# Experts with at most 32 tokens: four column quarters of TensorE in place of two halves

## The chip, the cores and the metric

One core of a Trainium2 chip runs the whole program in one launch. The metric is the device time of that launch in microseconds; the time before is the median of 3 runs. One further execution was recorded by the hardware profiler, and all rows below are from it.

## The reference, cut to what matters

Two layers, each a mixer and a feed-forward part, on 256 tokens of width 1024 in float32. The second layer's feed-forward part is a mixture of 8 experts with two chosen per token. The change touches that part alone:

```python
D_MODEL, SEQ, N_EXPERTS, TOP_K, D_FF_EXPERT = 1024, 256, 8, 2, 3584

def moe_swiglu(h, router_w, w_gate, w_up, w_down):
    logits = (xf @ router_w).astype(jnp.float32)
    top_val, top_idx = lax.top_k(logits, TOP_K)
    weights = jax.nn.softmax(top_val, axis=-1)
    ...
    def expert_block(args):
        toks, e = args
        xb = xf[toks]
        return (jax.nn.silu(xb @ w_gate[e]) * (xb @ w_up[e])) @ w_down[e]
    ...
    out = jnp.zeros((N, D), h.dtype).at[row_tok].add(y)
```

Each expert has 3 x 1024 x 3584 float32 weights, 44 MB; all eight are 352 MB, and every one of them is used in every launch.

## The kernel before, in words

`route` (L1090) computes the router's logits, the two chosen experts of each token, each token's place among its expert's tokens (`pos`, counted from 1, 0 where the expert is not chosen), its weight (`comb`) and the number of tokens of each expert (`cnt`). `moe` (L1219) does the rest.

**Steps.** The hidden width of 3584 is cut into ND = 7 pieces of 512, and a step (L1161) is one expert e and one piece d: first experts 0 to 3 for d = 0 to 6 in turn (28 steps: the first group), then experts 4 to 7 (the second group). Four steps of the same d are called a round here. A step needs six tiles of weights of 128 x 2048 float32 (1.0486 MB each): four "g" tiles (gate and up columns side by side: for each of 8 slices of the 1024 inputs and each half `ch` of the piece, 256 gate and 256 up columns) and two "d" tiles (down).

**Blocks.** Tokens of an expert are taken in blocks b of SL = 64; block 0 always runs, further ones under `tc.If(n_of[e] > 64 * b)`. n_of is the expert's count, loaded into registers of TensorE (PE), ScalarE (ACT) and VectorE (DVE) at d = 0 (L1404), behind the first `up` of that expert.

- `up` (L1265): for 8 slices kc and 2 halves ch, the gathered tokens (128 x 64, stationary) times 512 columns of a g tile, added up in one bank of PSUM. Half ch goes to partitions 64 ch to 64 ch + 63, so the two halves use different halves of the array's columns. 16 matmuls in float32, which the profile shows as 32 records. Then ACT computes Silu of the gate half, and DVE multiplies by the up half.
- `turn` (L1278): two transposes of 128 x 128 on PE and a copy by ACT, so that the hidden values lie with the piece's columns on the partitions.
- `down` (L1286): 8 matmuls (16 records) of these (128 x 64, stationary) by the d tiles, again in two halves of the array (n, the two halves of the 1024 outputs); DVE adds the result to `ya`, the expert's output so far.
- `gather` and `gather_more` (L1240, L1253) bring the expert's tokens together by matmuls with 0/1 matrices (`places`); `slots`, `weights` and `scatter` (L1305 to L1331) bring the outputs back at d = 6, with a matrix that holds `comb` at `pos`.

**Order.** The order of PE, ACT and DVE is the order of the program. Step i runs: `up(i, 0)`; `bring(i - 1)` (L1340), which is `down` of the step before, under `tc.If(n_of > 64)` with its further blocks and under `Else` alone; `turn(i, 0)`; then the further blocks' `up` under `tc.If` at L1424. An engine that skips a body takes a branch (COMPARE_BRANCH) and raises its semaphore by what the body would have (EVENT_SEMAPHORE), behind its own earlier work.

**Tiles.** `Stream` (L1164) loads the tiles on the queue of SyncE (SP) in the fixed order g(i), d(i - 1), g(i + 1), ... into 12 buffers (6 `wraw` and 6 `wmore`), which is two steps' worth. `used` (L1213) frees d(i - 1) behind `bring` and g(i) at the end of step i, behind L1424's body; then the next tiles are issued. So the six tiles g(i + 2) and d(i + 1) are issued at the end of step i, where PE's sequencer has passed L1424.

Of the kernel before, what the change touches and what calls it, by code (L numbers as in the profile page):

```python
# [27 lines left out]
NE = 8  # L28
# [11 lines left out]
def block_kernel(ctx, tc, x, cols, rows, ada_w, w_tok, w_in, cmp_w1, cmp_w2, w_out,  # L40
# [9 lines left out]
    def bank(tag, bufs):  # L50
        return pp.tile([128, 512], FT, name=tag, tag=tag, bufs=bufs)
# [7 lines left out]
    def tbank():  # L59
        return bank("tr", 2)  # L60

    def sbank():
        return bank("sc", 2)
# [196 lines left out]
    g = {}  # L260
# [829 lines left out]
    def route(mp, join, hT):  # L1090
        h2 = con.tile([128, 2, D], FT, name="h2", tag="hh")
        lgp = ring()

        def logits(t):
            for kc in range(KC):
                pe.matmul(lgp[:, t * 8:t * 8 + 8], hT[:, kc, t * 128:(t + 1) * 128], rw[:, kc],
                          start=kc == 0, stop=kc == KC - 1)

        def back(t):

            for n in range(2):
                ps = sbank()
                for c in range(4):
                    pe.transpose(ps[:, c * 128:(c + 1) * 128], hT[:, 4 * n + c, t * 128:(t + 1) * 128], ident)
                (act.copy, dve.tensor_copy)[n](h2[:, t, n * 512:(n + 1) * 512], ps)

        join.turn(0)
        join.total(1)
        join.hand(0)
        join.scale(1)  # L1110
        logits(0)
        back(0)
        join.turn(1)
        join.hand(1)
        logits(1)
        v8 = mp.tile([128, 2, 8], FT, name="v8")
        i8 = mp.tile([128, 2, 8], U32, name="i8")
        for t in range(2):
            lg = lgp[:, t * 8:t * 8 + 8]
            dve.max(v8[:, t], lg)  # L1120
            dve.max_index(i8[:, t], v8[:, t], lg)
        idf = mp.tile([128, 2, 8], FT, name="idf")
        dve.tensor_scalar(idf, i8, 1.0, None, op0=OP.add)
        four = [128, 2, 2, NE]
        oh = mp.tile(four, FT, name="oh")
        dve.tensor_tensor(oh, iota_f[:, None, None, 0:8].to_broadcast(four),
                          idf[:, :, 0:2, None].to_broadcast(four), op=OP.is_equal)
        routed = mp.tile([128, 2, NE], FT, name="routed")
        dve.tensor_tensor(routed, oh[:, :, 0], oh[:, :, 1], op=OP.add)
        back(1)  # L1130
        ps = ring()
        pv = ps[:, 0:32].rearrange("p (z t e) -> p z t e", z=2, t=2)
        pe.matmul(pv[:, 0], upper, routed, start=True, stop=False)
        pe.matmul(pv[:, 0, 1], ones, routed[:, 0], start=False, stop=False)
        pe.matmul(pv[:, 1], ones, routed, start=False, stop=True)
        ew = mp.tile([128, 2, 2], FT, name="ew")
        sw = mp.tile([128, 2], FT, name="sw")
        dve.tensor_tensor(ew, v8[:, :, 0:2], v8[:, :, 0:1].to_broadcast([128, 2, 2]), op=OP.subtract)
        act.activation(ew, ew, AF.Exp)

        pos = con.tile([128, 2, NE], FT, name="pos")
        dve.tensor_tensor(pos, pv[:, 0], routed, op=OP.mult)
        total = mp.tile([128, NE], FT, name="total")
        dve.tensor_copy(total, pv[:, 1, 0])
        dve.tensor_tensor(total, total, pv[:, 1, 1], op=OP.add)
        cnt = con.tile([1, NE], I32, name="cnt")
        dve.tensor_copy(cnt, total[0:1])
        comb = con.tile([128, 2, NE], FT, name="comb")

        def shares():  # L1150
            dve.tensor_tensor(sw, ew[:, :, 0], ew[:, :, 1], op=OP.add)
            dve.reciprocal(sw, sw)
            dve.tensor_tensor(ew, ew, sw[:, :, None].to_broadcast([128, 2, 2]), op=OP.mult)
            dve.tensor_tensor(oh, oh, ew[:, :, :, None].to_broadcast(four), op=OP.mult)
            dve.tensor_tensor(comb, oh[:, :, 0], oh[:, :, 1], op=OP.add)

        return h2, pos, comb, cnt, shares

    ND = FFE // 512

# [55 lines left out]
                    self.free[k] = True  # L1216
            self.pump()

    def moe(mp, stream, h2, pos, comb, cnt, shares):  # L1219
        engs = [EN.PE, EN.Activation, EN.DVE]  # L1220
        g2h = mp.tile([128, 512], FT, name="g2h")
        SL = 64
# [1 line left out]
        own = con.tile([128, 2, 2, 2, S], FT, name="own", tag="hl")  # L1224
        uown = own[:, 1].rearrange("p a b c -> p (a b) c")
        hown = con.tile([128, 4, S], FT, name="hown", tag="acc")
        gbank = [lambda: bank("g0", 1), lambda: bank("g1", 1)]
        ebank = [None, lambda: ybank(0), lambda: ybank(1), lambda: ybank(0)]

# [35 lines left out]
        def up(i, b):  # L1265
            e, d = STEPS[i]
            ps = ebank[b]() if b else gbank[i % 2]()
            for kc in range(KC):
                x = xs[e][:, kc, b * SL:(b + 1) * SL]
                for ch in range(2):  # L1270
                    pe.matmul(ps[ch * 64:ch * 64 + 64], x, stream.at["g", i, 2 * (kc // 4) + ch][:, kc % 4],  # L1271
                              start=kc == 0, stop=kc == KC - 1)
            h = hown[:, b] if b or i % 2 else mp.tile([128, 256], FT, name="hid")
            act.activation(h, ps[:, 0:256], AF.Silu)  # L1274
            dve.tensor_tensor(h, h, ps[:, 256:512], op=OP.mult)  # L1275
            hid[i, b] = h

        def turn(i, b):  # L1278
            ps = tbank()
            for f in range(2):  # L1280
                pe.transpose(ps[:, f * 128:(f + 1) * 128], hid[i, b][:, f * 128:(f + 1) * 128], ident)
            u = uown[:, b] if b or i % 2 else mp.tile([128, 256], FT, name="u")
            act.copy(u, ps[:, 0:256])
            us[i, b] = u.rearrange("p (f s) -> p f s", f=2)

        def down(i, b):  # L1286

            e, d = STEPS[i]
            ps = sbank()
            for ch in range(2):  # L1290
                for f in range(2):
                    for n in range(2):
                        pe.matmul(ps[n * 64:n * 64 + 64], us[i, b][:, f, ch * 64:ch * 64 + 64],  # L1293
                                  stream.at["d", i, ch][:, f, n * 512:(n + 1) * 512],
                                  start=ch + f == 0, stop=ch + f == 2)
            ya = yas[e][:, b]
            if d == 0:
                dve.tensor_copy(ya, ps)
            else:
                dve.tensor_tensor(ya, ya, ps, op=OP.add)  # L1300
            if d == ND - 1:
                dve.tensor_tensor(ya, ya, g2h, op=OP.mult)  # L1302


        def slots(e, b):  # L1305

            woh = mp.tile([128, 2, 2, SL], FT, name="woh")
            for t in range(2):
                dve.tensor_scalar(woh[:, t], iota_f[:, None, b * SL:(b + 1) * SL].to_broadcast([128, 2, SL]),
                                  pos[:, t, e:e + 1], comb[:, t, e:e + 1], op0=OP.is_equal, op1=OP.mult)  # L1310
            return woh

        def weights(e, b, woh):
# [26 lines left out]
        def bring(p):  # L1340

            e, d = STEPS[p]

            def back(b):
                if d == ND - 1:
                    scatter(e, b, 0, ybanks)
                    scatter(e, b, 1, sbanks)

            def more(b):
                turn(p, b)  # L1350
                down(p, b)
                back(b)

            with tc.If(n_of[e] > SL) as two:  # L1354
                turn(p, 1)
                down(p, 0)
                down(p, 1)
                back(1)
                beyond(e, more, 2)
            with two.Else():  # L1360
                down(p, 0)
            stream.used("d", p)

        def beside(i, b):

            e, d = STEPS[i]
            if d == ND - 1:
                woh = slots(e, b)
            up(i, b)
            if d == ND - 1:  # L1370
                weights(e, b, woh)

        def g2_row():
# [7 lines left out]
                          dg[:, 4 * n:4 * n + 4].rearrange("p a b -> p (a b)"), start=True, stop=True)  # L1381
            act.copy(g2h, ps)

        gather(0, places(0))
        shares()
        N = len(STEPS)
        done = None
        for i in range(N):
# [8 lines left out]
            if d == ND - 1:  # L1397
                if not e % 4:
                    wx = con.tile([128, 4, S], FT, name="wx", tag="xn0")
                woh = slots(e, 0)  # L1400
            if i < N - 1:
                up(i, 0)
            if d == 0:
                n_of[e] = nc.values_load(cnt[0:1, e:e + 1], engines=engs, min_val=0, max_val=S)  # L1404
            if i == 0:
                gather(2, oh)

# [4 lines left out]
            if i == 4 * ND:  # L1412
                oh = places(6)
            if i == N - 1:
                up(i, 0)
            turn(i, 0)
            if d == ND - 1:
                weights(e, 0, woh)
            if done is not None:
# [1 line left out]
                done = None  # L1421
            if i and STEPS[p][1] == ND - 1:
                done = STEPS[p][0]
            with tc.If(n_of[e] > SL):  # L1424
                if d == 0:
                    gather_more(e)
                beside(i, 1)
                beyond(e, lambda b: beside(i, b), 2)
            stream.used("g", i)
            if i == 5:  # L1430
                g2_row()
# [215 lines left out]
```

## Time and profile before

| | |
|---|---|
| median of 3 runs | 1604.83 us (1600.37 to 1605.38) |
| profiled execution: its time | 1605.7 us |
| its span, first to last instruction | 1604.0 us |
| TensorE matmul busy | 1461.9 us, 91% of the span, 7198 records |
| VectorE, ScalarE busy | 592.2 us (37%), 364.7 us (23%) |
| HBM read | 478.79 MB, 299 GB/s over the span |
| experts (L1219 on) | about 606 to 1604 us |

Instructions carry the kernel's line, their engine and the tiles that they write and read (out<-in). `wraw` and `wmore` are weight tiles, `x` the gathered tokens, `g` and `y` the PSUM banks of `up` for block 0 and for further blocks, `sc` that of `down`, `tr` that of `turn` (and of small products), `hid`, `hown` and `u`, `own` the hidden values before and after the turn. PEld is the loading of stationary operands. PEq is PE's sequencer: a wait that ends with it ends with a branch or a semaphore event there. The span's end follows the last tiles; matmul ends are modelled, and their starts are what to go by.

### The profile page before, as it was taken

How to read it: one execution, taken by the hardware profiler on the slowest of the kernel's cores; microseconds unless marked ns; L12 is line 12 of the kernel's file. 1: busy time of each engine (PE TensorE's matmuls, PEld its weight loads, DVE VectorE, ACT ScalarE, POOL GpSimd, SP SyncE). 2: the span in 40 equal slices, each digit the busy share in tenths (PEclk: the TensorE clock that was granted, in tenths of full speed). 3: DMA queues.
4: the chain of work that ended last, by engine and by line, in shares of the span. 5: the costliest groups of instructions: out<-in, count | busy, mean ns of one | idle time of the engine just before them, and what ended most of it. 6: DMA issues, size and time to landing. Idle time of an engine off the chain costs nothing. (4 is left out here: it accounts for less than half of the span.)

```text
span 1604.0 us, 18623 instructions
## 1 busy us (share of the span) xinstructions
PE 1461.9 (91%) x7198; PEld 791.7 (49%) x7198; DVE 592.2 (37%) x1097; ACT 364.7 (23%) x767; POOL 22.1 (1%) x62
## 2 busy tenths in 40 slices
PE   3999989999898999899999999998989999999985
PEld 3977767887787775233333333333333333333331
DVE  8868767877777751001010110113310100101123
ACT  2656453433574531000000000000000000000000
POOL 2000000000000000000000000000000000000000
PEclk9999999999999989999999999999999999999998
DMA  9745647777465353597889879786969999999992
GB/s 372 286 168 183 210 157 289 298 310 287 176 208 195 132 210 132 228 377 302 367 362 371 360 314 419 307 355 249 401 235 413 418 416 416 403 418 418 398 388 81
DMA packets 67452, 482.40 MB, mean 301 GB/s; under 512 B 7604, under 2 KB 7988, under 8 KB 9288
## 3 DMA queue, kind: packets, MB, share of 16 engines
q1 hardware_dynamic: 66800, 479.66, 75.3%
q8 instruction: 130, 2.13, 0.5%
q14 instruction: 50, 0.41, 0.1%
q10 hardware_dynamic: 472, 0.21, 0.0%
HBM read 478.79 MB, written 1.05 MB: 299 GB/s over the span
## 5 line engine op out<-in xcount | busy, mean ns | idle before, releaser
L1271 PE MATMUL g<-wraw,x 128*64 128x512 f32 x896 | 219.8, 606 | 23.3 <-PEq L1424 10.2
L1271 PE MATMUL g<-wmore,x 128*64 128x512 f32 x896 | 218.0, 600 | 18.6 <-DMA wmore<-in_moe_gu_w_dram 11.3
L1293 PE MATMUL sc<-wraw,own 128*64 128x512 f32 x768 | 172.3, 595 | 3.9 <-ACTq L1335 3.1
L190 DVE TENSOR_TENSOR wlo<-wraw,whi 128x2048 fp32r<-128x2048 f32 (+1 forms) x69 | 153.0, 2230 | 12.2 <-ACT whi L185 12.2
L1271 PEld LDWEIGHTS g<-wraw,x 128*64 128x64 f32 x896 | 73.8, 138 | 142.9 <-issue 121.6
L1271 PEld LDWEIGHTS g<-wmore,x 128*64 128x64 f32 x896 | 73.3, 138 | 141.5 <-issue 118.4
L185 ACT CAST whi<-wraw 128x2048 fp32r<-128x2048 f32 (+1 forms) x69 | 126.8, 1862 | 12.4 <-DMA wraw<-in_w_tok_dram 8.1
L379 PE MATMUL g<-whi,hh 128*128 128x512 f32 (+1 forms) x272 | 112.8, 415 | 8.2 <-DVE hh L371 7.7
L1300 DVE TENSOR_TENSOR ya<-ya,sc 128x512 f32<-128x512 f32 x66 | 45.4, 688 | 187.5 <-PE sc L1293 187.5
L380 PE MATMUL g<-whi,hl 128*128 128x512 f32 (+1 forms) x272 | 108.6, 399 | 0.9 <-DVE hl L372 0.9
L381 PE MATMUL g<-wlo,hh 128*128 128x512 f32 (+1 forms) x272 | 108.1, 397 | 0.3 <-DVE wlo L190 0.3
L1293 PE MATMUL sc<-wmore,u 128*64 128x512 f32 x432 | 107.2, 594 | 0.0
L1293 PEld LDWEIGHTS sc<-wraw,own 128*64 128x64 f32 x768 | 56.6, 137 | 102.5 <-issue 94.2
L1275 DVE TENSOR_TENSOR hown<-hown,g 128x256 f32<-128x256 f32 x28 | 11.8, 421 | 256.2 <-ACTq L1354 185.5
L224 DVE SCALAR_TENSOR_TENSOR acc<-wraw,csil,acc 128x1024 f32<-128x1024 f32 x82 | 105.2, 1283 | 2.2
L1275 DVE TENSOR_TENSOR hid<-hid,g 128x256 f32<-128x256 f32 x28 | 11.8, 421 | 199.4 <-ACT hid L1274 120.1
L379 PE MATMUL g<-hh,whi 128*128 128x256 f32 x256 | 74.7, 292 | 5.5 <-DVE x L526 5.0
L1271 PE MATMUL y<-wraw,x 128*64 128x512 f32 x336 | 76.4, 597 | 0.5 <-DVE ya L1300 0.5
L1271 PE MATMUL y<-wmore,x 128*64 128x512 f32 x336 | 75.7, 592 | 0.0
L380 PE MATMUL g<-hh,wlo 128*128 128x256 f32 x256 | 72.7, 284 | 0.6 <-DVE wlo L190 0.6
L381 PE MATMUL g<-hl,whi 128*128 128x256 f32 x256 | 72.6, 284 | 0.0
L1293 PEld LDWEIGHTS sc<-wmore,u 128*64 128x64 f32 x432 | 40.6, 137 | 56.4 <-issue 47.0
(347 smaller groups left out, 1643.7 us busy)
## 6 DMA issues: line engine op xcount, KB each, us to landing
wraw<-in_moe_gu_w_dram SPq DMA_DIRECT2D x112, 1024.0 KB, 10.3
wmore<-in_moe_gu_w_dram SPq DMA_DIRECT2D x112, 1024.0 KB, 11.2
wmore<-in_moe_d_dram SPq DMA_DIRECT2D x56, 1024.0 KB, 17.3
wraw<-in_moe_d_dram SPq DMA_DIRECT2D x56, 1024.0 KB, 19.8
wraw<-in_ada_w_dram SPq DMA_DIRECT2D x48, 1024.0 KB, 5.3
wraw<-in_w_in_dram SPq DMA_DIRECT2D x24, 1024.0 KB, 4.9
wraw<-in_ffn_gu_dram SPq DMA_DIRECT2D x22, 1024.0 KB, 5.4
wraw<-in_ffn_d_dram SPq DMA_DIRECT2D x11, 1024.0 KB, 4.9
```

The source lines that it names most:

```text
L185: act.copy(self.wh, self.v)
L190: dve.tensor_tensor(self.wl, self.v, self.wh.bitcast(FT), op=OP.subtract)
L224: dve.scalar_tensor_tensor(acc, v[:, o], sc, acc, op0=OP.mult, op1=OP.add)
L379: pe.matmul(ps, ah, bh, start=start, stop=False)
L380: pe.matmul(ps, al, bh, start=False, stop=False)
L381: pe.matmul(ps, ah, bl, start=False, stop=stop)
L1271: pe.matmul(ps[ch * 64:ch * 64 + 64], x, stream.at["g", i, 2 * (kc // 4) + ch][:, kc % 4], start=kc == 0, stop=kc == KC - 1)
L1275: dve.tensor_tensor(h, h, ps[:, 256:512], op=OP.mult)
L1293: pe.matmul(ps[n * 64:n * 64 + 64], us[i, b][:, f, ch * 64:ch * 64 + 64], stream.at["d", i, ch][:, f, n * 512:(n + 1) * 512], start=ch + f ...
L1300: dve.tensor_tensor(ya, ya, ps, op=OP.add)
```

## The change

The count of an expert selects between two forms of block 0, at run time and in every step. With more than 32 tokens the step is as before. With at most 32:

- `up_few`: the same 16 matmuls of 512 columns with 32 tokens as the stationary operand (128 x 32). Half ch and the parity of the slice kc choose one of four quarters of the array's columns, so even and odd slices add up in different partitions of the bank. ACT and DVE copy the bank's two halves to `hid` and `low`, without Silu and product.
- `turn_few`: four matmuls by `sel` (128 x 64, two identities of 32 for each half), which turn the values and add the even and the odd sums; then Silu and the product.
- `down_few`: 8 matmuls in four quarters (output half n, piece half ch); the two ch halves stay apart in `ya`, and the matrix of `slots` holds `comb` at `pos` and at `pos` + 32 (`pos2`), so that `scatter` adds them.

New control flow: `first` (If/Else around `up`), a second If/Else in `bring`, an If/Else around `turn` and L1424's body. The register load at d = 0 moves ahead of `up`. `turn` moves into the new If, behind `weights` and `scatter` in the steps that have them. Buffers, the order of the tiles and their release stay.

```diff
+        pos2 = con.tile([128, 2, NE], FT, name="pos2")
...
         def shares():
+
+            few = mp.tile([128, NE], FT, name="few")
+            dve.tensor_scalar(few, total, 32.0, 32.0, op0=OP.is_le, op1=OP.mult)
+            dve.tensor_tensor(pos2, pos, few[:, None, :].to_broadcast([128, 2, NE]), op=OP.add)
...
+        sel = mp.tile([128, 2, 32], FT, name="sel")
+        iv = ident.rearrange("p (c k s) -> p c k s", c=2, k=2)
+        dve.tensor_tensor(sel, iv[:, :, 0], iv[:, :, 1], op=OP.add)
...
-            h = hown[:, b] if b or i % 2 else mp.tile([128, 256], FT, name="hid")
+            h = hown[:, b] if b else hid[i, 0]
...
-            u = uown[:, b] if b or i % 2 else mp.tile([128, 256], FT, name="u")
+            u = uown[:, b] if b else uof[i]
...
+        def up_few(i):
+
+            e, d = STEPS[i]
+            ps = gbank[i % 2]()
+            for k in range(4):
+                for odd in range(2):
+                    kc = 2 * k + odd
+                    for ch in range(2):
+                        j = 2 * ch + odd
+                        pe.matmul(ps[32 * j:32 * j + 32], xs[e][:, kc, 0:32],
+                                  stream.at["g", i, 2 * (kc // 4) + ch][:, kc % 4], start=k == 0, stop=k == 3)
+            act.copy(hid[i, 0], ps[:, 0:256])
+            dve.tensor_copy(low[i], ps[:, 256:512])
+
+        def turn_few(i):
+
+            ps = tbank()
+            for c in range(4):
+                v = (hid[i, 0] if c < 2 else low[i])[:, c % 2 * 128:(c % 2 + 1) * 128]
+                pe.matmul(ps[:, 64 * c:64 * c + 64], v, sel.rearrange("p c s -> p (c s)"), start=True, stop=True)
+            u = uof[i][:, 0:128]
+            act.activation(u, ps[:, 0:128], AF.Silu)
+            dve.tensor_tensor(u, u, ps[:, 128:256], op=OP.mult)
+
+        def down_few(i):
+            e, d = STEPS[i]
+            ps = sbank()
+            u = uof[i][:, 0:128].rearrange("p (f c s) -> p f c s", f=2, c=2)
+            for f in range(2):
+                for n in range(2):
+                    for ch in range(2):
+                        j = 2 * n + ch
+                        pe.matmul(ps[32 * j:32 * j + 32], u[:, f, ch], stream.at["d", i, ch][:, f, n * 512:(n + 1) * 512],
+                                  start=f == 0, stop=f == 1)
+            gain(i, 0, ps)
...
@@ -1293,6 +1338,10 @@
                         pe.matmul(ps[n * 64:n * 64 + 64], us[i, b][:, f, ch * 64:ch * 64 + 64],
                                   stream.at["d", i, ch][:, f, n * 512:(n + 1) * 512],
                                   start=ch + f == 0, stop=ch + f == 2)
+            gain(i, b, ps)
+
+        def gain(i, b, ps):
+            e, d = STEPS[i]
...
-                dve.tensor_scalar(woh[:, t], iota_f[:, None, b * SL:(b + 1) * SL].to_broadcast([128, 2, SL]),
-                                  pos[:, t, e:e + 1], comb[:, t, e:e + 1], op0=OP.is_equal, op1=OP.mult)
+                for k in range(2):
+                    dve.tensor_scalar(woh[:, t, :, 32 * k:32 * k + 32],
+                                      iota_f[:, None, b * SL + 32 * k:b * SL + 32 * k + 32].to_broadcast([128, 2, 32]),
+                                      (pos2 if k > b else pos)[:, t, e:e + 1], comb[:, t, e:e + 1],
+                                      op0=OP.is_equal, op1=OP.mult)
...
-                down(p, 0)
+                with tc.If(n_of[e] > 32) as one:
+                    down(p, 0)
+                with one.Else():
+                    down_few(p)
...
+        def first(i):
+            with tc.If(n_of[STEPS[i][0]] > 32) as half:
+                up(i, 0)
+            with half.Else():
+                up_few(i)
...
-            if i < N - 1:
-                up(i, 0)
+            hid[i, 0] = hown[:, 0] if i % 2 else mp.tile([128, 256], FT, name="hid")
+            uof[i] = uown[:, 0] if i % 2 else mp.tile([128, 256], FT, name="u")
+            low[i] = mp.tile([128, 256], FT, name="low")
             if d == 0:
                 n_of[e] = nc.values_load(cnt[0:1, e:e + 1], engines=engs, min_val=0, max_val=S)
+            if i < N - 1:
+                first(i)
...
-            turn(i, 0)
+                first(i)
...
-            with tc.If(n_of[e] > SL):
-                if d == 0:
-                    gather_more(e)
-                beside(i, 1)
-                beyond(e, lambda b: beside(i, b), 2)
+            with tc.If(n_of[e] > 32) as half:
+                turn(i, 0)
+                with tc.If(n_of[e] > SL):
+                    if d == 0:
+                        gather_more(e)
+                    beside(i, 1)
+                    beyond(e, lambda b: beside(i, b), 2)
+            with half.Else():
+                turn_few(i)
```

## Rows read from the trace of the kernel before

**Rows 1.** windows: us, busy us (records) of PE, PEld, DVE, ACT, POOL, PEclk, DMA share, GB/s

```profile
606.00:671.00 65.00, 60.08 (x300) 26.00 (x298) 9.08 (x23) 7.03 (x16) 0.00 (x0) 1.00 0.41 163
671.00:1112.00 441.00, 411.95 (x1838) 147.60 (x1838) 54.19 (x103) 29.34 (x78) 0.00 (x0) 1.00 0.84 344
1112.00:1195.00 83.00, 75.19 (x374) 32.76 (x376) 20.18 (x38) 6.50 (x17) 0.00 (x0) 1.00 0.80 318
1195.00:1565.00 370.00, 346.02 (x1528) 124.69 (x1524) 42.75 (x79) 25.02 (x66) 0.00 (x0) 0.99 0.99 408
```

**Rows 2.** timeline, PE, one round: start, us, instruction, records, [idle <-releaser]

```profile
867.70 3.65 PE L1271 MATMUL g<-wmore,x 128*64 128x512 f32 x16 [0.45 <-PEq L1335]
...
874.72 0.44 PE L1281 MATMUL tr<-ident,hown 128*128 128x128 f32 x2
...
887.34 0.41 PE L1281 MATMUL tr<-ident,hid 128*128 128x128 f32 x2 [0.63 <-PEq L1335]
887.90 3.65 PE L1271 MATMUL g<-wraw,x 128*64 128x512 f32 x16
...
909.98 1.04 PE L1271 MATMUL g<-wraw,x 128*64 128x512 f32 x2 [0.15 <-PEq L1424]
911.50 3.22 PE L1271 MATMUL g<-wraw,x 128*64 128x512 f32 x13 [0.48 <-DMA wraw<-in_moe_gu_w_dram]
...
916.47 3.22 PE L1271 MATMUL g<-wmore,x 128*64 128x512 f32 x13 [1.31 <-DMA wmore<-in_moe_gu_w_dram]
...
923.48 0.44 PE L1281 MATMUL tr<-ident,hown 128*128 128x128 f32 x2
...
938.25 3.65 PE L1271 MATMUL g<-wmore,x 128*64 128x512 f32 x16 [0.44 <-PEq L1335]
```

**Rows 3.** timeline, the queue's issues of tiles in the same round

```profile
887.88 0.80 SPq L1201 DMA_DIRECT2D wmore<-in_moe_gu_w_dram  x2
...
909.95 0.80 SPq L1201 DMA_DIRECT2D wmore<-in_moe_gu_w_dram  x2
...
937.93 0.81 SPq L1201 DMA_DIRECT2D wraw<-in_moe_gu_w_dram  x2
...
958.38 0.80 SPq L1201 DMA_DIRECT2D wmore<-in_moe_gu_w_dram  x2
```

**Rows 4.** lines by form: shapes, records | busy us, mean ns | idle before

```profile
L1271 PE MATMUL g<-wraw,x 128*64 128x512 f32 x896 | 219.8, 606 | 23.3 <-PEq L1424 10.2 <-DMA wraw<-in_moe_gu_w_dram 9.0 <-issue 2.3
...
L1271 PE MATMUL y<-wraw,x 128*64 128x512 f32 x336 | 76.4, 597 | 0.5 <-DVE ya L1300 0.5
...
L1275 DVE TENSOR_TENSOR hown<-hown,g 128x256 f32<-128x256 f32 x28 | 11.8, 421 | 256.2 <-ACTq L1354 185.5 <-ACT hown L1274 70.7
...
L281 PE MATMUL tr<-dg,ones 128*128 128x512 f32 x8 | 3.8, 602 | 0.6 <-ACTq L1335 0.6
...
L618 PE MATMUL tr<-kc__323,qT 128*128 128x32 f32 x16 | 1.9, 270 | 0.0
...
L601 PE MATMUL tr<-hs,w 128*64 128x16 f32 x8 | 0.6, 220 | 0.0
```

**Rows 5.** timeline, PE: four records of 16 columns

```profile
137.31 0.29 PE L601 MATMUL tr<-hs,w 128*64 128x16 f32 x4
```

**Rows 6.** lines L1424 and L1404 on TensorE's sequencer: ns min/median/max, first and last start

```profile
L1424 PEldq COMPARE_BRANCH  x56: 70/382/4114, 616.1 to 1581.0; - x56
...
L1404 PEldq TENSOR_LOAD <-cnt x8: 299/309/489, 608.8 to 1199.0; - x8
L1404 PEldq FUSED_REGOPS  x8: 146/146/160, 609.4 to 1199.4; - x8
```

**Rows 7.** timeline, PE: first round, and where the second group settles

```profile
606.12 7.09 PE L1271 MATMUL g<-wraw,x 128*64 128x512 f32 x32
...
671.06 1.51 PE L1271 MATMUL g<-wraw,x 128*64 128x512 f32 x6 [3.11 <-PEq L1424]
...
1194.68 1.94 PE L1271 MATMUL g<-wraw,x 128*64 128x512 f32 x4 [3.89 <-PEq L1424]
```

More of the change, by code (lines that the diff above doesn't have):

```diff
@@ L1155, in shares @@
             dve.tensor_tensor(comb, oh[:, :, 0], oh[:, :, 1], op=OP.add)
-        return h2, pos, comb, cnt, shares
+        return h2, pos, pos2, comb, cnt, shares
     ND = FFE // 512
@@ L1217, in used, with moe @@
             self.pump()
-    def moe(mp, stream, h2, pos, comb, cnt, shares):
+    def moe(mp, stream, h2, pos, pos2, comb, cnt, shares):
         engs = [EN.PE, EN.Activation, EN.DVE]
@@ L1382, in g2_row @@
             act.copy(g2h, ps)
+        def first(i):
[3 more added lines that the diff above has]
+                up_few(i)
+        uof, low = {}, {}
         gather(0, places(0))
@@ L1414, in moe @@
             if i == N - 1:
-                up(i, 0)
-            turn(i, 0)
+                first(i)
             if d == ND - 1:
```

## The prediction

> **What bounds the kernel now.** The windows come first [rows 1]. Up to 606 us this is the mixer, the dense layer and the routing, which the change leaves alone; behind it are the experts. In 671 to 1112 (experts 0 to 3, d = 1 to 6) TensorE is busy 411.95 of 441 us and the transfers run at 344 GB/s; in 1195 to 1565 (experts 4 to 7, from d = 1 on) they run at 408 GB/s with a DMA share of 0.99. So the second group of experts waits for HBM, whatever TensorE does, and in the first TensorE looks like the bound.
>
> How many experts are "few"? The reference's router on its own inputs gives 14, 187, 27, 39, 11, 121, 55 and 58 tokens. The trace agrees: beside 2 x 896 matmul records for the first 64 tokens of all 56 steps stand 2 x 336 for further blocks [rows 4], that is 21 blocks of 32 records, 7 x (2 + 1): three blocks for expert 1 and two for expert 5. Experts 0, 2 and 4 are few: 21 steps of 56, and 14 of them in the first group.
>
> Now one round of the first group, expert by expert [rows 2, 3]. Steps end where the queue issues the next six tiles: expert 2 at 887.88, expert 1 at 937.93, expert 2 again at 958.38. A round takes 70.50 us. One tile takes 2.485 us: TensorE waited for the second and the fourth tile of one step until 911.50 and 916.47. So 24 tiles want 59.6 us, and the round has 10.9 us more. These lie where expert 1's three blocks hold their tiles until the step's end: after the issues at 909.95 the next is at 937.93. From 887.88 on, in contrast, the queue works through a chain of 12 tiles (gate/up of expert 0, down of 3, gate/up of 1, down of 0). Its tenth landed at 916.47, 28.59 us after the chain's start, so the twelfth lands at 28.59 + 2 x 2.485 = 33.56. Expert 1's step already waits for tiles (0.48 and 1.31 us): the half round from 887.88 to 937.93 is bound by transfers and by expert 1, the other (937.93 to 958.38, expert 2) by TensorE alone. That decides what a saving is worth.
>
> **The change part by part.** *Up.* 32 records stay 32, each with 512 columns. Today two halves of the array run side by side: 867.70 to 874.72, 7.0 us for 32 [rows 2], 0.22 each, against 3.8 us for 8 records over all 128 columns, 0.475 each [rows 4]. If four quarters run side by side as two halves do, 32 records take 3.5 us. No row shows quarters. Bounds: 3.5 us; 15.2 if they go one after another (32 x 0.475); 7.0 if only two go at a time. Issuing is not in the way: four small records of 0.22 us each took 0.29 together, so the last started 0.07 us behind the first [rows 4, 5], and 3.5 us leaves 0.11 for each. I take 3.5, since halving the columns has halved the time once: -3.5 per up, and -1.75 per down (16 records, 3.5 us now).
>
> [...]
>
> *Turn.* Two transposes (0.44 us with both) become four f32 matmuls, 8 records with full weights. Sixteen like them took 1.9 us [rows 4], so 8 take 1.0 to 1.1: +0.7. Bounds: 0 (hidden) and +1.8 (at half clock).
>
> *Branches.* Each step gains one If ahead of up, one in bring and one around turn. A branch on TensorE's sequencer takes 70 ns where it falls through, 382 at the median and up to 4114 [rows 6]; most of that lies under matmuls already queued, and the gaps it leaves are 0.15 to 0.63 [rows 2]. On the path stand the taken branch to up_few just behind a step's end (+0.3) and the jump over turn_few behind expert 1's blocks (+0.25). The branch to turn_few takes the place of L1424's, which stands at the same point today. Bounds: 0 where they lie under queued work, and for each of the two a stall like the 3.11 and 3.89 us of rows 7; I take the gaps of rows 2, which stand at the same places.
>
> *The register load* of the count moves ahead of up in eight steps. 0.31 + 0.15 us [rows 6] with an assertion and the issue between come to 0.75 as I take it (bounds 0.46 and twice that), now behind a step's end instead of under up's matmuls. In step 0 TensorE waits for the gathered tokens then, which hides it; in the others of a first round nothing does. ACT and DVE load it too and pass the new Ifs as well; behind these stand only Silu, product or copies, which wait for up anyway.
>
> *The rest.* ACT's Silu and DVE's product move behind the turn; in the few steps two copies stand in their place. Both engines are busy a tenth of the time (54.19 and 29.34 of 441 us [rows 1]), and the next up lies between turn_few and down_few. Where expert 1's turn waits for its hidden tile, down_few covers Silu and product (0.42 us for the product [rows 4], as much for Silu) with 1.75 us instead of 3.5; if that cover is short, a few tenths. Two operations for pos2, one for sel, two more per slots: on DVE, at its mean of 0.4 us [rows 1]; only sel stands ahead of the first gather (+0.2). SP's queue gets the same issues in the same order, released at the same step ends; POOL gets nothing.
>
> **The sum.** *Rounds d = 1 to 6 of the first group.* Expert 3's down of expert 2 is faster, expert 0's up too, but both stand between 887.88 and the twelfth tile and only lengthen TensorE's wait for tiles. Behind that tile: down_few cannot start before both down tiles are there (its loops take both in turn), so 33.56 + 1.75 = 35.3, against 923.48 - 887.88 = 35.6 today. Then the blocks of expert 1 as before, +0.25 for the jump: no gain down to 937.93. From there expert 2's step: -3.5 (up) + 0.7 (turn) + 0.3 (branch), and the chain starts that much earlier. Round: -0.3 + 0.25 - 2.5 = -2.5; six rounds: -15. That is a quarter of the 10.5 us that the matmuls save in each.
>
> *Round d = 0 (606.12 to 671.06, rows 7).* All tiles of two steps are there, TensorE is the bound: -3.5 - 1.75 - 3.5, + 1.4 (two turns) + 0.85 (branches) + 1.5 (loads in two steps) + 0.2 (sel) = -4.8.
>
> *Between the groups,* to 1194.68 where the second chain of transfers starts: down of 2 (-1.75), up and down of 4 (-5.25), + 0.7 + 0.55 + three loads (2.25) = -3.5. TensorE bounds it too (share 0.80, rows 1).
>
> *From there on* transfers bound it: 0. Expert 4's 5.25 us per round only become waits. What could be gained is the 0.01 of the DMA share.
>
> Sum: -15 - 4.8 - 3.5 = -23. The granted clock is 1.00 in the first group and 0.99 where TensorE waits for tiles [rows 1]; 0.01 of 441 us is 4.4 us of matmul time, most of it in waits, so I give back 1 (bounds 0 and 4.4): -22. The profiled execution took 1605.7 us (span 1604.0), 0.9 above the median of 1604.83; so 1583.7 on its own scale and about 1583 as a median.
>
> **The rivals.** *Half the array at a time.* If quarters share what two halves have, up_few takes 7.0 and down_few 3.5. Then the round pays: down_few waits for the second tile and ends at 37.1 (+1.5), turn +0.7, branches +0.55, so +2.8 x 6 = 17; round 0 +3.9, between the groups +3.5: 1605 + 24 = 1629. With u for the time of up_few a round changes by 1.5 u - 7.8 (up in expert 2's step, half of u in down_few), all stretches together by 13.5 u - 70, so this decides from u = 5.2 us on. For it: no row has four column groups. Against: two run at full speed. Chance 0.13. One after another (u = 15.2) it would be 1740: 0.02.
>
> *The whole saving counts.* If tiles were not waited for, a round would lose 10.5 us less 2, down to the 61 us that the transfers want: -9 x 6 - 8 - 7, 1536. For it: TensorE busy 93% of the stretch. Against: the waits for tiles in expert 1's step [rows 2], which grow when TensorE comes earlier. Chance 0.1.
>
> *Control flow eats it.* With three more branches a step and 56 more matmul records, each with its weight load, to run or to pass over, each of the two branches on the path costs about 1.3 us instead of 0.3, in six rounds and as much in the two stretches beside them: +2 x 8, which leaves -6 and 1599, or 1604 where two more stalls like the 3.11 us at 671.06 come in [rows 7]. [...] Chance 0.17.
>
> **Chances and range.** Forecast 0.55 (its own range 1572 to 1595), all of the saving 0.1, control flow 0.17, half the array 0.13, serial 0.02, the rest spread. A measurement of this kernel tells 0.3%, 4.8 us, from no change. Faster: 0.55 + 0.1 + a third of 0.17 = 0.71; same 0.1; slower 0.19. The range for 8 in 10 takes in control flow and half of the gap to each far case: 1557 to 1613.
>
> **What would show it.** Up_few's 32 records in 3.5 us (7.0: first rival). Rounds of 68.0 us in 671 to 1112, with TensorE's share there down to about 0.83 and waits for gate/up tiles several times today's; expert 2's step 18 us, expert 0 to 1 still 50. From 1195 on 408 GB/s as now. Gaps "PEq" ahead of the new Ifs under 0.5 us; over 1 us would speak for control flow. The prediction is wrong if the half round from the chain's start to expert 1's end gets shorter than 49 or longer than 52 us.

## The result, and the profile after

The changed kernel takes 1620.01 us (median of 4 runs, 1617.9 to 1623.28) against 1604.12 beside it: ratio 1.0108 [1.0095, 1.0121]. It is slower by 1%, where 1583 was forecast; the time lies outside the range. One execution of one run below, prime_early_short, took 2377.85 us at a granted clock of 0.557 and is left out of its median.

Windows of the changed kernel, with the columns of [rows 1]:

```profile
606.00:671.00 65.00, 60.35 (x322) 26.26 (x318) 7.62 (x16) 15.54 (x22) 0.00 (x0) 0.95 0.56 223
671.00:1112.00 441.00, 372.03 (x1930) 127.23 (x1926) 62.46 (x132) 109.98 (x143) 0.00 (x0) 0.95 0.85 344
1112.00:1195.00 83.00, 71.12 (x352) 30.37 (x350) 17.50 (x33) 19.77 (x26) 0.00 (x0) 0.94 0.73 293
1195.00:1565.00 370.00, 316.58 (x1480) 104.99 (x1478) 38.97 (x82) 98.80 (x121) 0.00 (x0) 0.95 0.96 391
```

Against [rows 1], TensorE is busy 40 us less in 671 to 1112, as forecast. But the transfers move no faster there (344 GB/s as before), they fall from 408 to 391 GB/s from 1195 on, where the old forms run, and ACT is busy nearly four times as long.

TensorE's timeline in expert 3's step at d = 1 and the start of the next step (start, us, records, idle before and what ended it): the last 16 records of `up` of expert 3, `down_few` of expert 2, then, behind the turn, `up_few` of expert 0 at d = 2.

```profile
740.29 3.60 PE L1280 MATMUL g<-wmore,x 128*64 128x512 f32 x16
746.34 1.92 PE L1327 MATMUL sc<-wmore,u 128*32 128x512 f32 x16 [2.44 <-DVE hown L1284]
...
752.33 3.31 PE L1304 MATMUL g<-wmore,x 128*32 128x512 f32 x16 [3.70 <-PEq L1490]
755.46 1.89 PE L1304 MATMUL g<-wraw,x 128*32 128x512 f32 x16
```

The quarters work: 16 records of `down_few` in 1.92 us, and 32 of `up_few` in 3.64 in the first step:

```profile
603.02 3.64 PE L1304 MATMUL g<-wraw,x 128*32 128x512 f32 x32
```

What is new is the idle time ahead of them. The branch behind the 3.70 us, by its line on the sequencer (ns min/median/max, first and last start), and the instruction queue in the microsecond at 749 (packets, MB, share of 16 engines):

```profile
L1490 PEldq COMPARE_BRANCH  x1: 4085/4085/4085, 747.5 to 747.5; - x1
```

```profile
q8 instruction: 1, 0.02, 4.9%
```

The jump over the further blocks' code starts at 747.51 and ends at 751.60. Meanwhile one packet of the instruction queue, 16,384 bytes of code, moves from 749.18 to 750.11; the jump ends 1.49 us behind it. (Ahead of `down_few` a jump of 5.99 us at L1413 ends at 746.07 in the same way, 1.51 us behind a packet; DVE's product, behind a table load, ends at 746.10.) So it is throughout: all 48 jumps over 0.7 us on TensorE's sequencer end 1.34 to 1.53 us behind the end of such a packet, and so do all 29 before (1.34 to 1.52). ACT and DVE pass the same 392 choices and need at most 74 ns for a jump.

The granted clock is lower as well. Behind the 3.70 us of idle time, the first 16 records of `up_few` take 3.31 us and the next 16 take 1.89. The windows of the two stretches, with the columns of [rows 1], show a granted clock of 0.50, then 1.00:

```profile
751.77:755.18 3.41, 2.85 (x16) 0.80 (x20) 0.00 (x0) 0.00 (x0) 0.00 (x0) 0.50 0.96 365
755.18:757.00 1.82, 1.82 (x20) 0.36 (x12) 0.00 (x0) 0.00 (x0) 0.00 (x0) 1.00 1.03 405
```

From 606 to 1565 us a clock of 0.50 was granted in 20 stretches, 95.6 us in sum, each of them beginning inside an idle time of TensorE of 1.3 to 5.9 us or up to 2 us behind it; before in 4, 13.7 us (idle times of 1.4 to 3.9 us). TensorE was busy in 82.3 us of the 95.6 (13.6 of the 13.7), so by estimate the lower clock took up to 41 us of matmul time (7 before).

The new branches over the whole program (compare [rows 6]; the old L1424 is now L1490):

```profile
L1488 PEldq COMPARE_BRANCH  x56: 65/70/4960, 608.3 to 1591.6; - x56
...
L1406 PEldq COMPARE_BRANCH  x56: 65/340/6180, 614.1 to 1599.0; - x56
...
L1413 PEldq COMPARE_BRANCH  x63: 65/176/5987, 614.5 to 1602.2; - x63
...
L1490 PEldq COMPARE_BRANCH  x56: 70/181/5323, 620.7 to 1598.2; - x56
```

Queues on the page of before, and of after (packets, MB, share):

```profile
q8 instruction: 130, 2.13, 0.5%
```

```profile
q8 instruction: 156, 2.56, 0.6%
```

All branches on TensorE's sequencer come to 392 and 218 us (before 182 and 81), those over 0.7 us to 158 us (47). And on ACT, by line from 606 to 1565 us:

```profile
L1283 ACT ACT_TABLE_LOAD x47 | 60.3, 1283 | 233.6 <-issue 119.2 <-PE g L1280 114.2
L1292 ACT ACT_TABLE_LOAD x43 | 55.2, 1283 | 79.6 <-PE tr L1290 79.2 <-ACTq L1406 0.2
L1316 ACT ACT_TABLE_LOAD x21 | 26.9, 1283 | 115.2 <-PE tr L1314 115.2
L1306 ACT ACT_TABLE_LOAD x19 | 24.4, 1283 | 93.8 <-PE g L1304 93.8
```

In the experts there are 147 loads of an activation table at 1.283 us, where before had one. Of these, 133 stand at lines of Silu (L1283, L1316) and of copies (L1292, L1306), on both sides of the choices.

Where the time went, from the start of each step's `up` in the trace (us). The stretches are the prediction's: d = 0 up to the start of step 3 (expert 3), d = 1 to 6 from there to the start of step 27 (expert 3 at d = 6), between from there to step 31, and the end from the last step on. The last two columns are TensorE's idle time from 606 us on, summed over gaps above 0.06 us: ended by a sequencer's branch or semaphore or by issue, and ended by a transfer.

| | to step 0 | d = 0 | d = 1 to 6 | between | from step 31 | end | span | sequencers | tiles |
|---|---|---|---|---|---|---|---|---|---|
| before | 606.1 | 64.9 | 445.0 | 78.6 | 378.2 | 31.1 | 1604.0 | 38.9 | 20.5 |
| after | 603.0 | 58.3 | 446.5 | 80.4 | 399.9 | 30.8 | 1618.9 | 101.7 | 4.1 |
| prime | 605.0 | 57.0 | 439.8 | 75.9 | 387.7 | 29.9 | 1595.2 | 103.4 | 5.0 |
| static | 602.5 | 58.6 | 428.2 | 73.7 | 376.7 | 29.9 | 1569.8 | 49.6 | 41.5 |
| never_prime | 603.9 | 65.0 | 467.4 | 79.4 | 390.6 | 29.9 | 1636.2 | 83.3 | 4.7 |
| before_short | 605.6 | 60.5 | 432.8 | 73.5 | 380.3 | 31.1 | 1583.9 | 17.4 | 25.9 |
| prime_short | 604.6 | 53.0 | 413.7 | 74.4 | 380.0 | 29.9 | 1555.7 | 34.6 | 36.2 |

The changed kernel gains 6.6 us at d = 0, nothing at d = 1 to 6, and loses 21.7 in the second group. (Step 0 itself starts between 602.5 and 606.1 us in these traces, behind work that no kernel changes.)

### The profile page after: what moved, and what is told of

Same layout as the page of the kernel before. It is cut to its first block, busy times and chain, and to the rows that moved or that the text cites. A ratio compares the mean times of both kernels' runs of the same rounds, so it can differ in the third digit from the quotient of the medians.

```text
span 1618.9 us, 19712 instructions
## 1 busy us (share of the span) xinstructions
PE 1402.7 (87%) x7324; PEld 752.9 (47%) x7324; DVE 602.1 (37%) x1143; ACT 550.7 (34%) x913; POOL 23.1 (1%) x62
## 5 line engine op out<-in xcount | busy, mean ns | idle before, releaser
L1280 PE MATMUL g<-wraw,x 128*64 128x512 f32 x544 | 145.0, 675 | 16.4 <-PEq L1490 12.7
L190 DVE TENSOR_TENSOR wlo<-wraw,whi 128x2048 fp32r<-128x2048 f32 (+1 forms) x69 | 153.0, 2230 | 12.2 <-ACT whi L185 12.2
L1280 PE MATMUL g<-wmore,x 128*64 128x512 f32 x576 | 132.5, 594 | 6.4 <-PEq L1387 3.1
L1338 PEld LDWEIGHTS sc<-wraw,own 128*64 128x64 f32 x768 | 53.2, 136 | 117.4 <-issue 104.9
L1280 PEld LDWEIGHTS g<-wraw,x 128*64 128x64 f32 x544 | 44.7, 154 | 98.8 <-issue 94.7
L1280 PEld LDWEIGHTS g<-wmore,x 128*64 128x64 f32 x576 | 43.3, 137 | 90.1 <-issue 85.4
L1292 ACT ACT_TABLE_LOAD x44 | 56.5, 1283 | 79.6 <-PE tr L1290 79.2
L1304 PE MATMUL g<-wmore,x 128*32 128x512 f32 x320 | 45.8, 681 | 32.1 <-PEq L1490 17.3
```

What stands on the lines that cost most here:

```text
L190: dve.tensor_tensor(self.wl, self.v, self.wh.bitcast(FT), op=OP.subtract)
L1304: pe.matmul(ps[32 * j:32 * j + 32], xs[e][:, kc, 0:32], stream.at["g", i, 2 * (kc // 4) + ch][:, kc % 4], start=k == 0, stop=k == 3)
```

## The experiments

Two theories at first: A, the control flow (choices that TensorE's sequencer passes); B, the table loads.

**prime**: the table loads away.

```
+        spare = mp.tile([128, 1], FT, name="spare")
+        act.activation(spare, mhalf[:, 0:1], AF.Silu)
         gather(0, places(0))
```

> The changed kernel with one Silu of a single column on ACT ahead of the first If, so that both sides of every If find the same activation table; the trace of the changed kernel has 147 table loads of 1.28 us in the experts, the one before has 1. Theory A (TensorE's sequencer: 392 branches in place of 182, 48 of them over 0.7 us, some 74 us of idle TensorE behind these against 10): the loads were mostly beside other work, so 1605 to 1614. Theory B (the table loads stretch the way from up over ACT and DVE to the turn, and that is what ate the gain): 1580 to 1592. Both: no table load inside the steps.

Measured 1604.79 us, ratio 1.0007 [0.9992, 1.0022], and no table load in any step. The loads cost the changed kernel some 15 us; without them it stands level with before, at the lower edge of A's range and far from B's.

**never_prime** and **never**: the choices alone.

```
-            with tc.If(n_of[STEPS[i][0]] > 32) as half:
+            with tc.If(n_of[STEPS[i][0]] > 0) as half:
```

(and so in the other two choices and in `few`; never_prime has the Silu above, never hasn't)

> The same, with the limit at 0 in place of 32 tokens, so that every step takes the form of before and the few forms are only passed over: the price of the control flow by itself, without table loads. Theory A: 15 to 30 us over the kernel before, 1620 to 1634, with branches of several us on TensorE's sequencer. Theory B: within 5 us of the kernel before, 1602 to 1609.

> As never_prime, without the Silu ahead, so with the table loads: their price by itself, in steps whose matmuls are those of before. Theory A: at most 10 us over never_prime, since a down of 3.5 us covers 1.28 + 0.38 + 0.42. Theory B: 25 to 35 us over it.

1638.72 us, ratio 1.0216 [1.0197, 1.0235], and 1643.07, 1.0257 [1.0227, 1.0287]. The same matmuls as before, with choices that always fall to the old form, cost 35 us: more than A said, and B is out. The loads add only 4.4 here.

**static**: the quarters without new choices.

```
-            with tc.If(n_of[STEPS[i][0]] > 32) as half:
-                up(i, 0)
-            with half.Else():
-                up_few(i)
+            (up_few(i) if STEPS[i][0] in FEW else up(i, 0))
```

(FEW = (0, 2, 4) in the program's text, likewise for turn and down: it serves these inputs' counts alone)

> The few forms with no new If: the kernel is written for the counts of these inputs, experts 0, 2 and 4 always few and the others never, so the choice at run time is left out; the Ifs on 64 tokens stay as before the change. Both theories, and the arithmetic of the prediction (half round of expert 0 to 1 held by tiles, 2.5 us less per round): 1580 to 1588, rounds of 68 us in the first group. If a round fell by 9 us instead, 1536: then the waits for tiles were misjudged.

1572.0 us, ratio 0.9798 [0.978, 0.9816]. The quarters win 31 us where nothing has to be chosen, more than the 1580 to 1588 that both theories gave. Its windows of 671 and 1195:

```profile
671.00:1112.00 441.00, 391.20 (x2016) 130.69 (x2008) 68.92 (x143) 29.96 (x83) 0.00 (x0) 0.99 0.88 359
...
1195.00:1565.00 370.00, 324.36 (x1519) 106.25 (x1518) 58.28 (x117) 26.81 (x73) 0.99 (x2) 1.00 0.93 382
```

So A holds, with a share for B, and the two nearly add up: 31 us gained (static) and 35 lost (never_prime) make 4 more than before, where prime has 2 more. Why do choices cost so much? A1: their number. A2: the code that a jump passes over.

**hollow**: never_prime with nearly empty Else sides.

```
             with half.Else():
-                up_few(i)
+                act.copy(spare, mhalf[:, 0:1])
```

(likewise for turn_few and down_few)

> As never_prime (every step runs the form of before, the Silu ahead of the first choice), with as many If/Else, but each Else, which never runs, holds a copy of one column on ACT in place of up_few, turn_few or down_few. Theory A1, the number of branches and joins costs: 30 to 38 us above before, as never_prime's 35.5. Theory A2, the code that a branch passes over costs: within 8 us of before.

**lumped**: the unused code in one block.

```
+            with tc.If(n_of[STEPS[i][0]] > 255):
+                up_few(i)
+                turn_few(i)
+                down_few(i)
             up(i, 0)
```

> Before (with the Silu ahead of the first choice), and at the start of each step one If that never runs, with up_few, turn_few and down_few of that step in it: never_prime's unused code, passed over by one branch a step where never_prime has three compares and three jumps. A1: 6 to 14 us above before. A2: 20 to 36 us above before.

**prime_short** and **before_short**: less of the old code.

```
-                if least < 3:
+                if least < 2:
                     beyond(e, f, least + 1)
```

> prime without the block for an expert's tokens 193 to 256 (no expert here has more than 187, so for these inputs nothing of the work is left out): a third of the code that experts with at most 64 tokens jump over is gone, and the number of jumps of these is the same. A1: 0 to 3 us below prime's 1604.8. A2: 8 to 25 us below prime.

> Before without the block for an expert's tokens 193 to 256 (none here has so many). A1: 0 to 2 us below before. A2: 2 to 10 us below before, so less than what prime_short gains on prime.

| | us | ratio to before | q8 packets |
|---|---|---|---|
| hollow | 1611.12 | 1.0034 [1.0021, 1.0046] | 132 |
| lumped | 1720.0 | 1.0725 [1.0695, 1.0756] | 155 |
| prime_short | 1556.21 | 0.9692 [0.9669, 0.9715] | 132 |
| before_short | 1583.99 | 0.9867 [0.9845, 0.9889] | 105 |

A1 is out: hollow has never_prime's 476 branches and 27.6 us less. The same line in both, never_prime first, then hollow:

```profile
L1492 PEldq COMPARE_BRANCH  x98: 65/184/5892, 614.0 to 1615.3; - x98
```

```profile
L1492 PEldq COMPARE_BRANCH  x98: 65/178/1934, 614.5 to 1589.3; - x98
```

The bytes passed over differ, and the longest jump of this line falls from 5.9 to 1.9 us; all jumps over 0.7 us come to 116 us in never_prime and to 32 in hollow. TensorE's semaphore events are not the cause: hollow has more of them in the experts, 358 against 273. (Its empty sides also write no PSUM bank; that was not tried by itself.) The short ones gained more than A2 had said, 48.6 us on prime and 21.2 on before, by taking away code that never ran (and 14 branches in expert 1's steps). Their packets fell by 24 and 25: the queue had moved that code all the same. In prime_short's timeline of the step shown above:

```profile
730.32 3.60 PE L1280 MATMUL g<-wmore,x 128*64 128x512 f32 x16
733.85 1.92 PE L1327 MATMUL sc<-wmore,u 128*32 128x512 f32 x16
...
737.05 1.92 PE L1304 MATMUL g<-wmore,x 128*32 128x512 f32 x16 [0.91 <-PEq L1492]
```

The 2.44 us ahead of `down_few` are gone (and the table load with them), the 3.70 ahead of `up_few` are 0.91. Per packet of code: never_prime to hollow 27.6 us for 24, before to before_short 21.2 for 25, prime to prime_short 48.6 for 24: 0.8 to 2.0 us each. The three later pairs, each with 24 packets less, gained more: 55.1 us (after_short), 57.8 (prime_early_short) and 70.2 (prime_else_short), 2.3 to 2.9 us a packet. lumped lost three times what never_prime does, beyond both expectations. Its long jump stands ahead of a step's first matmul, and that matmul, which shares a bank with the block, also waits for ACT and DVE to have passed it: their sequencers ended 53.5 us of TensorE's waits at the block's line, its own sequencer 70.2.

**after_short**: the change with its table loads, the code shortened in the same way.

> The changed kernel (with its table loads) without the block for an expert's tokens 193 to 256, which no expert here has. Against before_short (1584.0) it is the change with shorter code around it. If the code passed over was what ate the change: 1560 to 1572, that is 12 to 24 us below before_short, and 4 to 16 above prime_short's 1556.2 for the table loads. If the change loses by itself, whatever stands around it: 1590 or more.

1564.9 us, ratio 0.9746 [0.9722, 0.9771], as A2 had it: 19 us below before_short, 8.7 above prime_short. The change wins where the code around it is short.

**before_lean** and **lean**: `down(p, 0)` written once.

```
-            with tc.If(n_of[e] > SL) as two:
+            with tc.If(n_of[e] > SL):
                 turn(p, 1)
-                down(p, 0)
+            down(p, 0)
+            with tc.If(n_of[e] > SL):
                 down(p, 1)
                 back(1)
                 beyond(e, more, 2)
-            with two.Else():
-                down(p, 0)
```

> Before with down(p, 0) written once a step and not in both sides of a choice: the same work, right for any counts, eight matmuls of code fewer and one If more a step. A2, the code passed over costs: 3 to 14 us below before. A1, the number of branches costs: 0 to 4 us above.

> The change with the Silu ahead of the first choice, with up and the turn in quarters as before, but down in its old form for all (the turn leaves zeros in slots 32 to 63), written once a step: down_few, the second copy of down and one Else are gone from the code; right for any counts. It loses the 1.75 us that down_few saves in each step of experts 0, 2 and 4 where these are on the path. A2: 1578 to 1600, below before and below prime. A1: 1600 to 1612.

**lumped2**: lumped without the shared bank.

```
-            ps = gbank[i % 2]()
+            ps = gbank[(i + 1) % 2]()
```

> lumped with its unused up_few writing to the other accumulator bank, so that the first matmul of a step doesn't wait for ACT and DVE to pass the unused block. If that tie made lumped's 115 us: 1625 to 1655, as never_prime. If one long jump ahead of a step's first matmul makes it: 1690 to 1725.

before_lean 1632.46 us, 1.0183 [1.0156, 1.0211]; lean 1633.94, 1.02 [1.0156, 1.0243]; lumped2 1691.64, 1.0541 [1.0514, 1.0567]. The first two miss both expectations, on the slow side; lumped2 lies in the range given for the long jump. So A2 alone is not enough: before_lean has 7 packets fewer than before and lost 28 us. The tie of the banks was 28 of lumped's 115; its 87 left go with a long jump at the step's start. TensorE's waits in before_lean (us in total, times, longest):

```profile
PE g L1271 <- PEq L1423: 30.5, 25, 2.6
PE tr L1281 <- PEq L1357: 12.3, 40, 0.4
PE sc L1293 <- PEq L1354: 11.5, 39, 0.4
```

An If without Else that is passed over leaves a semaphore event behind the jump; of the 42 at L1424 in before, 37 start 0.04 to 0.14 us behind the end of TensorE's last matmul, and five later, 0.06 us behind a jump that ended after it. Before has 70 such events in the experts, before_lean 154. The matmuls next behind them were late by 35.1 us in sum before and by 79.2 here. Was it where the jump stands, then, and what work covers it (A3)?

**before_early**, **prime_early**, **prime_early_short**: both choices of a step straight behind `up`.

```
             up(i, 0)
             ...
+            with tc.If(n_of[e] > SL):
+                ...
+            down(p, 0)
             turn(i, 0)
-            with tc.If(n_of[e] > SL):
-                ...
```

> Before with both choices of a step (expert p's further blocks, then expert i's) straight behind up(i, 0), and down(p, 0) and the turn behind them: the same work and the same two choices a step, right for any counts. In before the second choice stood behind the short turn, with the next step's up waiting for it. A3, a jump costs what the array has no matmuls left to cover: 1580 to 1597. A2, only the code that is passed over counts: 1598 to 1606.

> The same order with the change (and the Silu ahead of the first choice): the choice of up's form, then the two choices of further blocks, then down and the turn with their choices. Right for any counts. A3: 1560 to 1592, below prime's 1605. A2: 1598 to 1610.

> prime_early without the block for tokens 193 to 256, which no expert here has: a candidate beyond prime_short's 1556. A3: 1545 to 1560, little below prime_short, since there the jumps were nearly covered. A2: 1550 to 1560.

before_early 1642.98 us, 1.0253 [1.0236, 1.027]; prime_early 1617.85, 1.0087 [1.007, 1.0104]; prime_early_short 1560.1, 0.973 [0.9711, 0.9749]. The first two miss A3's ranges and A2's as well, on the slow side, the third lies just above both. A3 in this form is out. TensorE's waits in before_early point to why: if the first choice's semaphore event waits until `up` has ended, as those at L1424 in before do for the last matmul, the second jump begins with nothing left to cover it.

```profile
PE sc L1293 <- PEq L1415: 44.3, 23, 3.2
PE sc L1293 <- ACTq L1335: 12.4, 21, 0.7
PE sc L1293 <- DVEq L1354: 11.2, 9, 1.5
```

A4 therefore: that wait is what costs.

**before_else**, **prime_else**, **prime_else_short**: no choice without an Else in a step.

```
-            turn(i, 0)
             ...
-            with tc.If(n_of[e] > SL):
+            with tc.If(n_of[e] > SL) as half:
+                turn(i, 0)
                 ...
+            with half.Else():
+                turn(i, 0)
```

> Before, with turn(i, 0) moved into both sides of a step's second choice (more than 64 tokens: the turn and the further blocks; Else: the turn alone), so that no choice of a step is passed over without an Else; the same work, right for any counts, two matmuls of code more a step. A4, an If without Else makes TensorE's sequencer wait for its own last matmul, and the next matmul comes late by that and the jump (18.8 us at 42 such places in the trace of before): 1580 to 1597. A2, only the code passed over counts: 1602 to 1612.

> The change with the Silu ahead of the first choice and the same edit: more than 64 tokens: the turn and the further blocks; Else: the choice between turn and turn_few. Right for any counts. In prime's trace the matmuls behind its 21 Ifs without Else were late by 40.8 us in sum. A4: 1560 to 1590. A2: 1600 to 1612.

> prime_else without the block for tokens 193 to 256, which no expert here has. In prime_short's trace the matmuls behind the 21 Ifs were late by 19.3 us in sum. A4: 1538 to 1552. A2: 1554 to 1562.

before_else 1609.76 us, 1.0034 [1.001, 1.0058]; prime_else 1627.17, 1.015 [1.0115, 1.0186]; prime_else_short 1556.99, 0.971 [0.969, 0.9729]. A4 missed all three; A2's ranges hold before_else and prime_else_short, but not prime_else. The waits went (42 of the 70 in before_else, and the 21 of prime's steps in prime_else), but the long jumps stayed, up to 6.06 us against 6.14 in prime. The line in prime, then in prime_else, and there TensorE's waits:

```profile
L1492 PEldq COMPARE_BRANCH  x56: 70/181/6137, 621.3 to 1574.4; - x56
```

```profile
L1490 PEldq COMPARE_BRANCH  x56: 70/1645/6057, 609.0 to 1595.6; - x56
```

```profile
PE tr L1314 <- issue: 28.6, 10, 4.1
PE g L1304 <- issue: 23.9, 8, 4.8
PE tr L1290 <- issue: 23.9, 7, 6.5
```

TensorE's idle time that ended with "issue" rose from 51 us in prime to 99, while "PEq" fell from 38 to 7: what the waits gave up came back, and more. In the changed kernel the starts of the queue's packets in the experts lie 6.4 us apart at the median, 4.4 at the tenth percentile and never under 3.1. Whether that distance is what the "issue" time waits for was not shown.

**What is settled and what is open.** Shown by taking code away: the price goes with the code that jumps pass over (hollow, and five pairs with and without the block for tokens 193 to 256). Not settled is the price of one jump in its place. The waits behind an If without Else fit the losses of before_lean, lean and before_early; yet taking them away gained nothing in before_else and prime_else. What starts the next packet was not tried, nor what of the price comes with the clock: from 606 to 1565 us a clock of 0.50 was granted for 122.9 us in prime_else and 47.8 in never_prime, against 13.7 in hollow and 23.0 in prime_short. The fastest is prime_short, 1556.21 us (prime_else_short, 1556.99, is level with it), below both kernels and below static; like all the "short" ones it serves experts with at most 192 tokens. No run that serves any counts beats before: prime, level with it, is the best.

## Why the prediction was wrong

- **Quarters side by side: right.** 32 records in 3.64 us against 3.5, 16 in 1.92 against 1.75, so the rivals of half the array and of a serial array are out.
- **The sum over the matmuls: right, and rather low.** static against before, from the stage table: -16.8 at d = 1 to 6 (forecast -15), -6.3 at d = 0 (-4.8), -4.9 between the groups (-3.5), -1.5 from there on (0). The half round to expert 1's end stays bound as forecast: 51.3 us before and 51.5 in static as a mean of six; expert 2's step falls from 22.9 to 19.8, as a mean of d = 1 to 6.
- **The failed step: *Branches*.** "I take the gaps of rows 2, which stand at the same places": +0.3 and +0.25 on the path. The choices cost 35 us (never_prime), and 27.6 of them go with the code in their unused sides. The gaps of [rows 2] belonged to the old code; with 26 more packets of code the packets start elsewhere and closer together (6.4 us apart at the median, before 7.5), and the steps that got shorter have less time for each. The rows to take were in the prediction: 4114 ns [rows 6] and the 3.11 and 3.89 us of [rows 7], which I had called two stalls more.
- **"From there on transfers bound it: 0."** The largest loss is here, 21.7 us, in steps of which only expert 4's change: the new code stands in all of them, and the transfers fall to 391 GB/s, as I read it since tiles are freed late. Of the 21.7, 12.2 go with the table loads (prime loses 9.5 here).
- **The second failure: *The rest*.** For ACT it counted the moved Silu and a copy, and no table loads; these cost some 15 us (prime).
- **The clock in the sum** was "I give back 1 (bounds 0 and 4.4)", with the clock of before. With the jumps and their idle time the granted clock averaged 0.95 there, up to 41 us of matmul time by the estimate above; static, without the choices, kept 0.99 and 1.00 in the two long stretches.
- **The rival "control flow eats it" had the direction and not the size**: two branches a round at 1.3 us in the first group, for 1599 to 1604. prime, at 1604.79, is there, but by a wider loss: against static 11.6 us at d = 1 to 6 and 11.0 from step 31 on. No run shows the 1.3 us; in the changed kernel 344 of the 392 jumps took at most 0.45 us and the other 48 took 3.3 us on average (158 us in sum).
- **The signs.** TensorE's share of 671 to 1112 fell to 0.84, as forecast (0.83), for another reason: tile waits fell from 20.5 to 4.1 us instead of growing severalfold. The half round reached 57.9 us in one round and 48.6 in another, both beyond the 49 to 52 named as the mark of an error; but that mark was too narrow, since two of the six half rounds of before already took 53.2 and 52.4. The granted clock averaged 0.95 in place of 1.00 from 671 to 1112, where TensorE now stood idle for up to 5.9 us at a time (before at most 3.1).

## What to carry to other kernels

Price a run-time choice by the code that it adds and passes over, counted in the packets of the instruction queue, and not by the branch's median: here 0.8 to 2.9 us for each packet of 16 KB, in every step and also where the old form runs. Split a change with a choice into two runs, the choice made in the program's text (the gain) and the choice that always falls to the old form (the price), before believing either. Look at the activation functions on both sides of a choice: here Silu on one and copies on the other came with 147 table loads of 1.283 us, some 15 us of the time (prime).

## What the runs showed of the hardware

- Four column groups of 32 in float32 ran side by side: 32 records in 3.64 us, 0.114 each, against 0.22 in halves and 0.475 over all columns [rows 4].
- A jump on TensorE's sequencer takes 65 ns to 6.2 us in the changed kernel. Those over 0.7 us end 1.34 to 1.53 us behind a packet of 16,384 bytes on its instruction queue, and the queue also moves the code that is passed over (24 or 25 packets less where code that never ran was taken out).
- Behind the 3.70 us of idle time at 748.6 to 752.3, TensorE ran at a granted clock of 0.50 until 755.18: 16 records in 3.31 us, then 16 in 1.89.
- Code that never ran cost before 21 us (before_short), 1.3% of its time.
- One Silu of one column ahead of the first choice removed all 147 table loads from the experts (prime).
